# Weight sums by accumulating transfers in two of four query and key steps, and the gate's upper norm ahead of the first step

## The chip, the cores and the metric

The kernel runs on one core of one Trainium2 chip. The metric is the device time of one execution in microseconds, as the median of several runs. One execution was also taken with the hardware profiler; its rows give the times of single instructions.

## The reference

A decoder block on 1024 tokens of width 1024, all in float32. The part around the change is the first projection and what follows it:

```python
xn = rmsnorm(h, norm_mix_g[layer])
proj = xn @ w_in[layer]                       # 1024 x 2568
q, k, v = ...                                 # 512 columns each
log_f = log_sigmoid(proj[..., G_END:] + b_forget[layer])   # 8 columns
att = forgetting_attention(q, k, v, log_f)
uv = gelu(proj[..., V_END:G_END])             # u and vg, 512 columns each
vg = rmsnorm(vg, v_gain)                      # in groups of 64 columns
sg = u * (causal 128x128 mix of vg + b_s)
h = h + concat(att, sg) @ w_out
h = h + conv_ffn(rmsnorm(h, norm_ffn_g), ...) # up, causal depthwise conv, silu gate, down
return rmsnorm(h, norm_final_g)
```

## The kernel before

**Products.** Every large matrix product is cut into 2 x 2 blocks and done with seven block products instead of eight (Strassen-Winograd). The blocks of the weights are called A11, A12, A21, A22 and their sums S1 to S4; those of the activations B11, B21, B22 and T1 to T4. A value that enters a product is split into a high part (a cast on ScalarE) and the rest (a subtraction on VectorE), and a product adds three matmul passes: high by high, high by rest, rest by high. So each weight block or sum costs one operation on ScalarE and one on VectorE before TensorE can use it (`tsplit`). The split tiles lie in a ring of six buffers (two "wy", four "whl").

**Order of the first stages.** u, the gate and the values of the lower 512 tokens are projected first (to about 104 us). Then come four steps of queries and keys, `qk_step(0..3)`, each for 128 columns of q and k, with the forget columns (`forget`, `forget_sums`) between, and after them the upper values, the spatial gate and attention. In a step TensorE runs the products S2, S3, A12 (A11 came in the step before), S1, A22 and S4 (L400, `product`), and VectorE combines the banks qa to qd. S3 and A22 add up in one bank (qc), S1 and S4 in another (qd): the second product of a bank can start only when VectorE has read the first out of it. `emit` scales, splits and stores q and k.

**Weights of a step.** `Weights(i)` loads four blocks of 128 x 512 into two "raw" tiles (of four): `a` holds the blocks 2 and 3 (A11, A12), `b` the blocks 0 and 1 (A21, A22). `sums` makes on GpSimd S3 = A21 + A11 over A11, S2 = S3 + A22 in a "gg" buffer (of two) and S1 = A21 + A22 over A21; `last_sum` makes S4 = S2 + A12 over A12. A sum in place must wait until the block it overwrites has been split. The generator `nxt_of(i)` does this for step i + 1 in the course of step i.

**The gate.** `vgt[0]` and `vgt[1]` hold the gate of the first and of the last 512 tokens ("lower" and "upper" half), each as four tiles of 128 tokens by 512 columns. `gate_part(i)` squares two of the four tiles (ScalarE) and sums the squares over groups of 64 (VectorE) in step i; the second part of a half (i = 1 and i = 3) also takes root and reciprocal and multiplies the half, 2048 wide (tile names G and gms in the profile). `gate_gain` multiplies a half by the gain (G and gg): the upper one in step 3, the lower one after the steps. The gain is loaded into a "gg" buffer and stays there until both are done.

**Values.** After the steps, `wvr[k]` loads the value weights into "raw" tiles as W2 and W3 leave them, and L684 adds the two blocks of each on GpSimd.

**What sets the order.** ScalarE and VectorE keep the written order up to `values_low(3)`. From there a planner orders the instructions of each engine and queue: it goes by their place in the program and by when, by its own costs, their operands and buffers come free. The order on each engine is then fixed. A queue (SP's for loads and stores, GpSimd's) stands still at an instruction whose operands aren't there, and all behind it waits.

In the profile, operations of ScalarE and VectorE in this stage all have the line L43, that of a helper; they are told apart by their tiles (raw and gg into wy or whl: splits; pt: squares and `xu`; qa to qd: banks).

Of the kernel before, what the change touches and what calls it, by code (L numbers as in the profile page):

```python
# [12 lines left out]
ALU = mybir.AluOpType  # L13
AX = mybir.AxisListType
P = 128
# [49 lines left out]
def block_kernel(ctx: ExitStack, tc: tile.TileContext, xT, xtok, wuv, wv, wqk, wf, cpk, bfv,  # L65
                 ggain, g2r, gfr, wsp, woa, wos, wup, wdn, out):
    nc = tc.nc
    act, dve, pool, pe, sp = Line(nc.scalar, tc), Line(nc.vector, tc), Line(nc.gpsimd, tc), nc.tensor, nc.sync
# [13 lines left out]
    def nm(s):  # L82
        uid[0] += 1
        return f"{s}_{uid[0]}"
# [6 lines left out]
    def sb(tag, shape, dt=F32):  # L91
        return (raws if tag == "raw" else late if tag in LATE else early).tile(shape, dt, tag=tag, bufs=BUFS[tag], name=nm(tag))
# [7 lines left out]
    def sbank():  # L100
        return psa.tile([P, 512], F32, tag="s", name=nm("ps"))

    def f32(ap):
        return ap.bitcast(F32)
# [92 lines left out]
    def ring(dt=F32R):  # L197
        rn[0] += 1
        return sb(RTAG[(rn[0] - 1) % 6], [P, 2, 512], dt)

    def psq(tag):
        return psa.tile([P, 512], F32, tag="b" if tag in "ab" else "s", bufs=4, name=nm("q" + tag))
# [29 lines left out]
    for p_ in range(2):  # L232
        t = sb("G", [P, 2, 2, 512])
# [3 lines left out]
    vgt = [sb("G", [P, 4, 512]) for _ in range(2)]  # L237
# [21 lines left out]
    def tprod(banks, src, n, first, neg=False):  # L259
        for k in range(4):  # L260
            tmul(banks, tsplit(src(k), neg), n, k, first)
# [67 lines left out]
    for j in range(2):  # L329
        g = gb[2 * j:2 * j + 2]  # L330
# [3 lines left out]
    for j in range(2):  # L334
        t1, t2, t3 = tmp[j]
        for c in range(2):
            k = 2 * j + c
# [27 lines left out]
    for j in range(2):  # L365
        t2 = tmp[j][1]
        for c in range(2):
            k = 2 * j + c
# [26 lines left out]
    def product(ps, w, n, first):  # L395
        c = 0
        for k in range(4):
            ks = slice(k * P, (k + 1) * P)
            for wi, xi in ((0, 0), (0, 1), (1, 0)):
                pe.matmul(ps, w[:, wi, ks], xs(n, xi, k), start=(first and c == 0), stop=(c == 11),  # L400
                          skip_group_check=True)
                c += 1

    class Weights:


        def __init__(self, i):
            self.a, self.b = sb("raw", [P, 2, 512]), sb("raw", [P, 2, 512])
            sp.dma_start(out=self.a, in_=wqk[i, :, 2:4, :])
            sp.dma_start(out=self.b, in_=wqk[i, :, 0:2, :])  # L410
            self.w = {}
            self.src = {"A11": self.a[:, 0, :], "A12": self.a[:, 1, :], "A22": self.b[:, 1, :]}
# [5 lines left out]
        def sums(self):  # L418

            a11, a21, a22 = self.a[:, 0, :], self.b[:, 0, :], self.b[:, 1, :]  # L420
            s2_ = sb("gg", [P, 512])
            pool.tensor_tensor(out=a11, in0=a21, in1=a11, op=ALU.add)
            pool.tensor_tensor(out=s2_, in0=a11, in1=a22, op=ALU.add)
            pool.tensor_tensor(out=a21, in0=a21, in1=a22, op=ALU.add)
            self.src.update({"S3": a11, "S2": s2_, "S1": a21})

        def last_sum(self):

            a12 = self.a[:, 1, :]
            pool.tensor_tensor(out=a12, in0=self.src["S2"], in1=a12, op=ALU.add)  # L430
            self.src["S4"] = a12

    W = [Weights(0)]
# [54 lines left out]
    def forget_sums(c, r, zr):  # L488
        sel, bfb, z, e, rows = c[0:64, 128:136], c[:, 136:144], c[:, 144:208], c[:, 208:272], c[0:64, 272:400]
        tri, ones, lh, ll = r[:, 0:P], r[:, P:2 * P], r[:, 256:320], r[:, 320:384]  # L490
        v3 = lambda t: t.rearrange("p (h t) -> p h t", h=8)
        ps = sbank()
        for tt in range(8):
            pe.matmul(ps[:, tt * 8:(tt + 1) * 8], zr[:, tt * P:(tt + 1) * P], sel, start=True, stop=True)
        dve.tensor_tensor(out=v3(z), in0=ps[:, 0:64].rearrange("p (t h) -> p h t", h=8),
                          in1=rstd1.unsqueeze(1).to_broadcast((P, 8, 8)), op=ALU.mult)
        dve.tensor_tensor(out=v3(z), in0=v3(z), in1=bfb.unsqueeze(2).to_broadcast((P, 8, 8)), op=ALU.add)
        dve.scalar_tensor_tensor(out=e, in0=z, scalar=-1.0, in1=z, op0=ALU.mult, op1=ALU.max)
        act.activation(e, e, AF.Exp, scale=-1.0)
        act.activation(e, e, AF.Ln, bias=one[:, 0:1])  # L500
        dve.tensor_scalar(out=z, in0=z, scalar1=-1.0, scalar2=0.0, op0=ALU.mult, op1=ALU.max)
        dve.tensor_tensor(out=z, in0=z, in1=e, op=ALU.add)
        dve.tensor_copy(lh, z)
        dve.tensor_tensor(out=ll, in0=z, in1=f32(lh), op=ALU.subtract)

        for o, m in ((64, tri), (128, ones)):
            pe.matmul(ps[:, o:o + 64], m, lh, start=True, stop=False)
            pe.matmul(ps[:, o:o + 64], m, ll, start=False, stop=True)
        whole, run = v3(ps[:, 128:192]), v3(e)
        dve.memset(run[:, :, 0:1], 0.0)  # L510
        for tt in range(1, 8):
            dve.tensor_tensor(out=run[:, :, tt:tt + 1], in0=run[:, :, tt - 1:tt], in1=whole[:, :, tt - 1:tt], op=ALU.add)
        dve.tensor_tensor(out=v3(z), in0=v3(ps[:, 64:128]), in1=run, op=ALU.add)
        pe.transpose(ps[0:64, 192:320], z, ident)
        act.activation(rows, ps[0:64, 192:320], AF.Copy, scale=-1.0)
        sp.dma_start(out=ncd.rearrange("h (t p) -> (h t) p", p=P), in_=rows)
# [12 lines left out]

    gms = cst.tile([P, 64], F32, name="gms")  # L530

    def gate_part(i):

        hf, t = 1 - i // 2, 2 * (i % 2)
        sq = sb("pt", [P, 2, 512])
        act.activation(sq, vgt[hf][:, t:t + 2, :], AF.Square)
        r = gms[:, hf * 32 + t * 8:hf * 32 + t * 8 + 16]
        dve.tensor_reduce(out=r, in_=sq.rearrange("p t (g d) -> p (t g) d", d=64), axis=AX.X, op=ALU.add)
        if t:
            r = gms[:, hf * 32:hf * 32 + 32]  # L540
            act.activation(r, r, AF.Sqrt, bias=eps[:, 0:1], scale=1.0 / 64)
            dve.reciprocal(r, r)
            v3 = vgt[hf].rearrange("p t (g d) -> p (t g) d", d=64)
            dve.tensor_tensor(out=v3, in0=v3, in1=r.unsqueeze(2).to_broadcast((P, 32, 64)), op=ALU.mult)

    def nxt_of(i):
        if i == 3:
# [13 lines left out]
    def qk_step(i, qa, nxt):  # L561
        w, t = W[i], xu[i]
        x1, u2 = t[:, 0, :], t[:, 1, :]
        qb = psq("b")
        product(qb, w.w["S2"], "T2", True)
        next(nxt)
        dve.tensor_tensor(out=u2, in0=qb, in1=x1, op=ALU.subtract)
        qc = psq("c")
        product(qc, w.w["S3"], "T3", True)
        dve.tensor_tensor(out=tk[:, 1, hi], in0=u2, in1=qc, op=ALU.subtract)  # L570
        w.split("S1")
        if i > 0:
            product(qa, w.w["A12"], "B21", False)
            act.copy(tq[:, 1, lo], qa)
        else:
            dve.tensor_tensor(out=tq[:, 1, lo], in0=q2, in1=x1, op=ALU.add)
        emit(tq, qd, i, -0.125, (lo,))
        w.split("A22")
        if i == 3:
            gate_gain(1)  # L580
        qd_ = psq("d")
        product(qd_, w.w["S1"], "T1", True)
        dve.tensor_tensor(out=tk[:, 1, hi], in0=tk[:, 1, hi], in1=qd_, op=ALU.subtract)
        gate_part(i)
        product(qc, w.w["A22"], "T4", False)
        dve.tensor_tensor(out=tk[:, 1, lo], in0=u2, in1=qc, op=ALU.subtract)
        emit(tk, kd, i, 1.0, (lo, hi))
        qa = next(nxt)
        w.split("S4")
        next(nxt)  # L590
        product(qd_, w.w["S4"], "B22", False)
        dve.tensor_tensor(out=tq[:, 1, hi], in0=qd_, in1=u2, op=ALU.subtract)
        emit(tq, qd, i, -0.125, (hi,))
        return qa

    gg = []

    def gate_gain(hf):
        if not gg:
            gg.append(sb("gg", [P, 512]))  # L600
            sp.dma_start(out=gg[0], in_=ggain.to_broadcast((P, 512)))
        dve.tensor_tensor(out=vgt[hf], in0=vgt[hf], in1=gg[0].unsqueeze(1).to_broadcast((P, 4, 512)), op=ALU.mult)

    W[0].split("S2", "S3")
    forget_sums(*fg)
    for i in range(4):
        qa = qk_step(i, qa, nxt_of(i))
# [2 lines left out]
    wvr = []  # L610
    for k in range(4):
        t = sb("raw", [P, 2, 512])
        sp.dma_start(out=t, in_=wv[k])
        wvr.append(t)


# [25 lines left out]
    for p_ in range(2):  # L642
        t = ring(F32)
# [37 lines left out]
    S = [sbank() for _ in range(4)]  # L681
    for k in range(4):
        tmul(S, w0[k], "T3", k, True)
        pool.tensor_tensor(out=wvr[k][:, 1, :], in0=wvr[k][:, 0, :], in1=wvr[k][:, 1, :], op=ALU.add)  # L684
    tprod(S, lambda k: wvr[k][:, 1, :], "B22", False)
    spatial()
    for m in range(4):
# [495 lines left out]
    for p_, n in ((upl, "B11"), (upl, "T2"), (upl, "B21"), (upl, "T3"), (upr, "T1"), (upr, "T4"), (upr, "B22")):  # L1183
        t = ut_(p_, "x" + n, [P, 2, 4, 512], F32, 1)
# [37 lines left out]
    def blk(b):  # L1222
        return lambda p_: wd[p_][:, b, :]
# [129 lines left out]
```

## Time and profile before

| | us |
|---|---|
| median of 3 runs | 1100.56 (1096.5 to 1100.8) |
| the profiled execution, its own time | 1103.27 |
| its span, first to last instruction | 1101.5 |
| TensorE busy with matmuls | 1073.1 (97%) |
| VectorE busy | 900.0 (82%) |
| ScalarE busy | 572.7 (52%) |
| GpSimd busy | 249.2 (23%) |

The four steps lie at 118.4, 137.8, 156.8 and 176.1 us, the upper values from 200.2 us. A row of a timeline gives the start, the length (of all that it holds), the engine, the line, what is written and read, how often, and in brackets the idle time before it with what ended it. The release that it names is the one that came last by the profile; where that can't be the reason, the program tells which it was. A product's twelve matmuls overlap, so the distance from one product's start to the next one's is its price, not the length in the row.

### The profile page before, as it was taken

How to read it: one execution, taken by the hardware profiler on the slowest of the kernel's cores; microseconds unless marked ns; L12 is line 12 of the kernel's file. 1: busy time of each engine (PE TensorE's matmuls, PEld its weight loads, DVE VectorE, ACT ScalarE, POOL GpSimd, SP SyncE). 2: the span in 40 equal slices, each digit the busy share in tenths (PEclk: the TensorE clock that was granted, in tenths of full speed). 3: DMA queues.
4: the chain of work that ended last, by engine and by line, in shares of the span. 5: the costliest groups of instructions: out<-in, count | busy, mean ns of one | idle time of the engine just before them, and what ended most of it. 6: DMA issues, size and time to landing. Idle time of an engine off the chain costs nothing.

```text
span 1101.5 us, 14438 instructions
## 1 busy us (share of the span) xinstructions
PE 1073.1 (97%) x5013; PEld 881.8 (80%) x5013; DVE 900.0 (82%) x1355; ACT 572.7 (52%) x991; POOL 249.2 (23%) x205
## 2 busy tenths in 40 slices
PE   9999999999998999988999999999999999999997
PEld 6888787777887888766888888888888888888886
DVE  5985799775678977999798989999998876898774
ACT  6656544454468865653444444444444454454653
POOL 0002243133035331334232423333232000000000
PEclk9999999899999999999999999999999999999999
DMA  9242366846548345113123232313321899433342
GB/s 339 85 153 78 100 169 181 231 140 209 189 133 268 98 144 188 70 67 134 68 105 134 78 114 96 124 68 123 116 96 45 270 330 324 122 97 101 124 137 96
DMA packets 64714, 158.18 MB, mean 144 GB/s; under 512 B 7673, under 2 KB 7937, under 8 KB 64641
## 3 DMA queue, kind: packets, MB, share of 16 engines
q1 hardware_dynamic: 64352, 156.70, 42.5%
q8 instruction: 39, 0.64, 0.2%
q10 hardware_dynamic: 288, 0.56, 0.1%
q14 instruction: 35, 0.28, 0.1%
HBM read 114.95 MB, written 42.27 MB: 143 GB/s over the span
## 4 chain that ended last, share of the span: by engine, by line
PE 67%; DVE 7%; ACT 3%; DMA 2%; issue 2%; POOL 1%; SPq 0%; DVEq 0%; ACTq 0%; POOLq 0%
PE k L1210 18%; PE qd L1020 10%; PE qa L1020 10%; PE qc L1020 9%; PE qb L1020 5%; PE pb L794 2%; PE ps L256 2%; PE pb L784 2%; PE pf L824 1%; PE pf L823 1%; PE pf L825 1%; DVE whb L159 1%; DMA rsd<-t 1%; PE ps L759 1%; PE ps L758 1%
## 5 line engine op out<-in xcount | busy, mean ns | idle before, releaser
L1210 PE MATMUL k<-whb,wha 128*128 128x512 f32 x924 | 209.6, 389 | 0.0
L1210 PEld LDWEIGHTS k<-whb,wha 128*128 128x128 f32 x924 | 173.4, 188 | 36.1
L1020 PE MATMUL qa<-xB,wha 128*128 128x512 f32 x528 | 129.4, 395 | 5.7 <-DVE wha L159 5.7
L1020 PE MATMUL qc<-xT,whb 128*128 128x512 f32 x540 | 130.3, 390 | 1.7 <-DVE xT L951 1.3
L1020 PEld LDWEIGHTS qa<-xB,wha 128*128 128x128 f32 x528 | 100.2, 190 | 27.3 <-DVE wha L159 6.5
L1020 PEld LDWEIGHTS qc<-xT,whb 128*128 128x128 f32 x540 | 101.1, 188 | 23.8 <-DVE xT L951 1.8
L153 ACT CAST wha<-sg 128x512 fp32r<-128x512 f32 x77 | 47.9, 622 | 97.3 <-PE k L1210 87.1
L153 ACT CAST whb<-sg 128x512 fp32r<-128x512 f32 x85 | 52.0, 616 | 70.3 <-PE qc L1020 67.7
L159 DVE TENSOR_TENSOR wha<-sg,wha 128x512 fp32r<-128x512 f32 x77 | 52.9, 689 | 42.5 <-ACT wha L153 42.4
L159 DVE TENSOR_TENSOR whb<-sg,whb 128x512 fp32r<-128x512 f32 x85 | 63.0, 742 | 8.9 <-ACT whb L153 8.7
L1020 PE MATMUL qd<-xB,whb 128*128 128x512 f32 x264 | 64.6, 393 | 0.1
L794 PE MATMUL pb<-pt,V 128*128 128x256 f32 (+1 forms) x320 | 60.1, 301 | 4.6 <-ACT pt L785 4.0
L1020 PE MATMUL qd<-xT,whb 128*128 128x512 f32 x264 | 63.4, 389 | 0.0
L1020 PE MATMUL qb<-xT,whb 128*128 128x512 f32 x252 | 61.0, 389 | 1.0 <-DVE whb L159 1.0
L794 PEld LDWEIGHTS pb<-pt,V 128*128 128x128 f32 x320 | 48.0, 192 | 16.6 <-ACT pt L785 11.4
L785 ACT CAST pt<-pb 128x512 fp32r<-128x512 f32 (+1 forms) x80 | 41.0, 543 | 36.7 <-PE pb L784 36.0
L786 DVE TENSOR_TENSOR pt<-pb,pt 128x512 fp32r<-128x512 f32 (+1 forms) x80 | 48.6, 634 | 13.3 <-ACT pt L785 12.8
L1020 PEld LDWEIGHTS qd<-xB,whb 128*128 128x128 f32 x264 | 50.2, 190 | 11.0 <-issue 0.5
L1020 PEld LDWEIGHTS qd<-xT,whb 128*128 128x128 f32 x264 | 49.6, 188 | 10.3
L908 POOL TENSOR_TENSOR sg<-sg,raw 128x512 f32<-128x512 f32 x21 | 42.8, 2038 | 64.7 <-issue 61.3
L907 POOL TENSOR_TENSOR sg<-raw 128x512 f32<-128x512 f32 x21 | 30.7, 1460 | 112.7 <-DVE whb L159 103.4
L1020 PEld LDWEIGHTS qb<-xT,whb 128*128 128x128 f32 x252 | 47.2, 188 | 11.2 <-DVE whb L159 1.4
(391 smaller groups left out, 2310.8 us busy)
## 6 DMA issues: line engine op xcount, KB each, us to landing
raw<-wup SPq DMA_DIRECT2D x44, 512.0 KB, 3.6
sg<-hx SPq DMA_DIRECT2D x77, 256.0 KB, 3.0
hx<-hs SPq DMA_DIRECT2D x44, 256.0 KB, 2.0
hx<-ca SPq DMA_DIRECT2D x33, 256.0 KB, 2.2
xT<-wdn SPq DMA_DIRECT2D x28, 256.0 KB, 5.3
raw<-wqk SPq DMA_DIRECT2D x8, 512.0 KB, 3.3
qd<-G SPq DMA_DIRECT2D x16, 256.0 KB, 3.3
kd<-G SPq DMA_DIRECT2D x16, 256.0 KB, 3.2
```

Source lines behind the costliest of these rows:

```text
L153: act.copy(h, src)
L159: return eng.tensor_tensor(out=l, in0=src, in1=f32(h), op=ALU.subtract)
L256: pe.matmul(banks[m], xs(n, xi, k)[:, ms], w[:, wi, :], start=(first and k == 0 and c == 0), stop=(k == 3 and c == 2), skip_group_check=True)
L758: pe.matmul(ps[:, 0:e - c], A[:, qs], B[:, c:e], start=True, stop=False)
L784: pe.transpose(ptr[:, c:c + P], tj[jj][:, k * P:(k + 1) * P], ident)
L785: act.copy(pt[:, 0, 0:w], ptr[:, 0:w])
L786: dve.tensor_tensor(out=pt[:, 1, 0:w], in0=ptr[:, 0:w], in1=f32(pt[:, 0, 0:w]), op=ALU.subtract)
L794: pe.matmul(po[:, oo:oo + n], lhs, pt[:, s, o:o + n], start=(k == 0 and s == 0), stop=(s == 1 and half))
L907: pool.tensor_tensor(out=s[0], in0=a21, in1=a22, op=ALU.add)
L908: pool.tensor_tensor(out=s[1], in0=s[0], in1=a11, op=ALU.add)
L1020: pe.matmul(ps, w[:, wi, ks], xb[:, xi, k, :], start=(first and n == 0), stop=(n == 11), skip_group_check=True)
L1210: pe.matmul(banks[bk + m], xh[:, xi, ms], wh[:, wi, :], start=(first and p_ == 0 and n == 0), stop=(p_ == NP - 1 and n == 2), skip_group_c ...
```

## The change

- In steps 2 and 3 the weight sums aren't made by GpSimd's adds. S2's buffer is loaded with block 2 by a plain transfer from SP's queue, and transfers issued by GpSimd add block 0 and block 1 to it, block 1 to A21 (S1) and block 0 to A11 (S3), all from memory. S4 is made by a transfer that adds S2, from one buffer to the other, to A12. Steps 0 and 1 keep the adds.
- The upper value sums are made by an accumulating transfer behind each load, instead of L684.
- The upper half's two gate parts (with its norm) stand ahead of step 0, before `forget_sums`; the lower half's stand in the steps 0 and 1 instead of 2 and 3. The gain of the upper half stands in step 2 instead of 3.
- The multiplications by norm and gain are cut into two pieces of 1024 each.

```diff
         def __init__(self, i):
-            self.a, self.b = sb("raw", [P, 2, 512]), sb("raw", [P, 2, 512])
+            self.i, self.a, self.b = i, sb("raw", [P, 2, 512]), sb("raw", [P, 2, 512])
...
             s2_ = sb("gg", [P, 512])
-            pool.tensor_tensor(out=a11, in0=a21, in1=a11, op=ALU.add)
-            pool.tensor_tensor(out=s2_, in0=a11, in1=a22, op=ALU.add)
-            pool.tensor_tensor(out=a21, in0=a21, in1=a22, op=ALU.add)
+            if self.i < 2:
+                pool.tensor_tensor(out=a11, in0=a21, in1=a11, op=ALU.add)
+                pool.tensor_tensor(out=s2_, in0=a11, in1=a22, op=ALU.add)
+                pool.tensor_tensor(out=a21, in0=a21, in1=a22, op=ALU.add)
+            else:
+                blk = lambda b: wqk[self.i, :, b, :]
+                sp.dma_start(out=s2_, in_=blk(2))
+                for t, b in ((s2_, 0), (a21, 1), (s2_, 1), (a11, 0)):
+                    pool.dma_start(out=t, in_=blk(b), accum_op=ALU.add)
             self.src.update({"S3": a11, "S2": s2_, "S1": a21})
...
             a12 = self.a[:, 1, :]
-            pool.tensor_tensor(out=a12, in0=self.src["S2"], in1=a12, op=ALU.add)
+            if self.i < 2:
+                pool.tensor_tensor(out=a12, in0=self.src["S2"], in1=a12, op=ALU.add)
+            else:
+                pool.dma_start(out=a12, in_=self.src["S2"], accum_op=ALU.add)
...
-    def gate_part(i):
-
-        hf, t = 1 - i // 2, 2 * (i % 2)
+    def gate_part(hf, t):
+
         sq = sb("pt", [P, 2, 512])
...
-            v3 = vgt[hf].rearrange("p t (g d) -> p (t g) d", d=64)
-            dve.tensor_tensor(out=v3, in0=v3, in1=r.unsqueeze(2).to_broadcast((P, 32, 64)), op=ALU.mult)
+            for t in (0, 2):
+                v3 = vgt[hf][:, t:t + 2, :].rearrange("p t (g d) -> p (t g) d", d=64)
+                dve.tensor_tensor(out=v3, in0=v3, in1=r[:, t * 8:t * 8 + 16].unsqueeze(2).to_broadcast((P, 16, 64)),
+                                  op=ALU.mult)
...
         w.split("A22")
-        if i == 3:
-            gate_gain(1)
         qd_ = psq("d")
         product(qd_, w.w["S1"], "T1", True)
         dve.tensor_tensor(out=tk[:, 1, hi], in0=tk[:, 1, hi], in1=qd_, op=ALU.subtract)
-        gate_part(i)
+        if i < 2:
+            gate_part(0, 2 * i)
+        elif i == 2:
+            gate_gain(1)
...
-        dve.tensor_tensor(out=vgt[hf], in0=vgt[hf], in1=gg[0].unsqueeze(1).to_broadcast((P, 4, 512)), op=ALU.mult)
+        for t in (0, 2):
+            v = vgt[hf][:, t:t + 2, :]
+            dve.tensor_tensor(out=v, in0=v, in1=gg[0].unsqueeze(1).to_broadcast((P, 2, 512)), op=ALU.mult)

     W[0].split("S2", "S3")
+    gate_part(1, 0)
+    gate_part(1, 2)
     forget_sums(*fg)
...
         sp.dma_start(out=t, in_=wv[k])
+        pool.dma_start(out=t[:, 1, :], in_=wv[k, :, 0, :], accum_op=ALU.add)
         wvr.append(t)
...
         tmul(S, w0[k], "T3", k, True)
-        pool.tensor_tensor(out=wvr[k][:, 1, :], in0=wvr[k][:, 0, :], in1=wvr[k][:, 1, :], op=ALU.add)
```

## The prediction

> **What bounds the kernel now.** I read the page first, then the stage that the diff touches: a table by steps, TensorE's waits there, and the order of time on each engine.
>
> ```profile
> span 1101.5 us, 14438 instructions
> PE 1073.1 (97%) x5013; PEld 881.8 (80%) x5013; DVE 900.0 (82%) x1355; ACT 572.7 (52%) x991; POOL 249.2 (23%) x205
> ```
>
> TensorE is busy 97% of the span, so only what shortens its path counts: 28 us are idle, and some matmuls run slowly. The windows view (span; busy time and count of PE, PEld, DVE, ACT, POOL; granted clock; DMA share; GB/s), cut at the first matmul of the steps 1, 2, 3 and of the value products:
>
> ```profile
> 137.80:156.80 19.00, 19.00 (x85) 15.73 (x84) 17.48 (x23) 8.80 (x15) 8.21 (x4) 1.00 0.59 158
> 156.80:176.10 19.30, 19.30 (x86) 15.69 (x85) 17.92 (x19) 6.84 (x12) 9.78 (x6) 1.00 0.55 154
> 176.10:200.20 24.10, 19.29 (x74) 15.15 (x73) 22.21 (x27) 12.81 (x23) 4.47 (x3) 0.87 0.70 201
> 200.20:222.50 22.30, 22.30 (x98) 18.45 (x97) 14.78 (x22) 8.75 (x14) 3.37 (x5) 0.98 0.86 254
> ```
>
> Steps 1 and 2 are full of matmuls. Step 3 takes 24.10 us for fewer of them (74), at a clock of 0.87, with VectorE busy 22.21 of 24.10 us. So the loss is in step 3 and VectorE is late there. TensorE's waits from 104 to 225 us (line, releaser: total, times, longest) hold nothing else of size:
>
> ```profile
> PE qd L400 <- ACT G L43: 4.1, 1, 4.1
> PE ps L507 <- DVE gg L43: 0.8, 1, 0.8
> PE qc L400 <- DVE G L43: 0.7, 1, 0.7
> ```
>
> The timeline of PE (start, length, group, and in brackets the idle time before it):
>
> ```profile
> 156.81 2.88 PE L400 MATMUL qb<-H,whl 128*128 128x512 f32 x12
> ...
> 176.09 2.88 PE L400 MATMUL qb<-H,wy 128*128 128x512 f32 x12
> 178.81 2.88 PE L400 MATMUL qc<-x,wy 128*128 128x512 f32 x12
> ...
> 184.25 2.88 PE L400 MATMUL qd<-H,whl 128*128 128x512 f32 x12
> 187.84 2.96 PE L400 MATMUL qc<-V,whl 128*128 128x512 f32 x12 [0.71 <-DVE G L43]
> 194.91 5.46 PE L400 MATMUL qd<-t,whl 128*128 128x512 f32 x12 [4.11 <-ACT G L43]
> 200.17 6.00 PE L256 MATMUL ps<-wy,x 128*128 128x512 f32 x24
> ```
>
> A product follows the one before after 178.81 - 176.09 = 2.72 us. Step 3 has six products (S2, S3, A12, S1, A22, S4), 16.32 us, and takes 200.17 - 176.09 = 24.08. The 7.76 us of loss lie in three places: A22 starts 187.84 - 184.25 - 2.72 = 0.87 late, S4 starts 194.91 - 187.84 - 2.72 = 4.35 late, and S4 itself, after that idle time, takes 200.17 - 194.91 = 5.26, so 2.54 too long. What S4 waited for is on VectorE:
>
> ```profile
> 180.48 1.22 DVE L43 TENSOR_REDUCE gms<-pt 128x16 f32<-128x1024 f32 x1 [0.27 <-ACT pt L43]
> ...
> 182.21 0.34 DVE L43 RECIPROCAL gms<-gms 128x32 f32<-128x32 f32 x1
> ...
> 183.02 2.28 DVE L43 TENSOR_TENSOR G<-G,gms 128x2048 f32<-128x2048 f32 x1
> ...
> 187.01 0.68 DVE L43 TENSOR_TENSOR G<-pt,qc 128x512 f32<-128x512 f32 x1
> 187.61 2.67 DVE L43 SCALAR_TENSOR_TENSOR wy<-raw,wy 128x512 fp32r<-128x512 f32 x2
> 190.20 2.28 DVE L43 TENSOR_TENSOR G<-G,gg 128x2048 f32<-128x2048 f32 x1
> 192.40 1.77 DVE L43 SCALAR_TENSOR_TENSOR G<-G,t 128x512 f32<-128x512 f32 x1
> 194.09 0.67 DVE L43 TENSOR_TENSOR G<-G,qd 128x512 f32<-128x512 f32 x1
> 194.69 0.68 DVE L43 SCALAR_TENSOR_TENSOR whl<-raw,whl 128x512 fp32r<-128x512 f32 x1
> ```
>
> S4 accumulates on bank qd, which the subtraction at 194.09 must have read: it ends at 194.76, and S4 starts 0.15 later. The wait view names ScalarE because a cast ended last; the program says VectorE. A22 likewise stands behind the subtraction of qc at 187.01. VectorE has no gap in this stretch, so these two reads are late by whatever stands ahead of them: the gate's second norm (reduction, reciprocal, multiplication), and adds of GpSimd beside them:
>
> ```profile
> 142.39 3.37 DVE L43 TENSOR_TENSOR G<-G,gms 128x2048 f32<-128x2048 f32 x1
> ```
> ```profile
> 143.57 3.35 POOL L424 TENSOR_TENSOR raw<-raw 128x512 f32<-128x512 f32 x1
> ...
> 151.40 1.61 POOL L430 TENSOR_TENSOR raw<-gg,raw 128x512 f32<-128x512 f32 x1 [4.48 <-DVE wy L43]
> ...
> 188.19 1.55 POOL L654 TENSOR_SCALAR_AFFINE_SELECT pt<-pt 128x1024 f32<-128x1024 f32 x1
> 192.35 1.26 POOL L684 TENSOR_TENSOR raw<-raw 128x512 f32<-128x512 f32 x1 [2.62 <-DMA raw<-wv]
> ```
>
> The same multiplication took 3.37 us beside the add at 143.57 and 2.28 without one: 1.09 more. GpSimd's add suffers too, 3.35 us there and 1.26 at 192.35. The operation at 192.40 (1.77, where the one at 194.69 takes 0.68) pays the same 1.09, beside the add at 192.35.
>
> **The change part by part.** *Step 3's norm goes.* The part of the gate that ran in step 3 now runs in step 1, and the upper half's norm runs ahead of step 0. Out of step 3 go 1.22 + 0.34 + 2.28 = 3.84 us of VectorE. *Its adds go:* L684 becomes four transfers, so the operation at 192.40 is 1.09 shorter. The two splits at 187.61 (2.67 for two of 0.68) may gain up to 1.3, but the select at 188.19 stays beside them, and I take 0. The subtraction of qd then starts at 194.09 - 3.84 - 1.09 = 189.16, ends at 189.83, and S4 may start at 189.98. A22 no longer waits: 184.25 + 2.72 = 186.97, to 189.69. So S4 is still 0.29 late. A gap of 0.87 cost its product 0.08 (2.96 against 2.88), so I take 0.1 for its clock. S4 ends at 189.98 + 2.72 + 0.1 = 192.8 instead of 200.17: **7.4 us gained**. Next to be late is VectorE again; the value products behind S4 are fed by splits that come the same 4.93 us earlier.
>
> *The norm in front* adds, ahead of step 0, one more square on ScalarE, a reduction, a root with its table load, a reciprocal and the multiplication. One reduction ran there already:
>
> ```profile
> 112.17 1.22 DVE L43 TENSOR_REDUCE gms<-pt 128x16 f32<-128x1024 f32 x1 [0.70 <-ACT pt L43]
> ...
> 120.41 0.23 DVE L43 TENSOR_TENSOR gg<-ps,rstd 128x64 f32<-128x64 f32 x1 [3.91 <-PE ps L494]
> ```
> ```profile
> 111.08 1.06 ACT L43 ACTIVATE pt<-G 128x1024 f32<-128x1024 f32 x1 [0.34 <-issue]
> ...
> 121.10 1.28 ACT L43 ACT_TABLE_LOAD   x1
> ```
>
> On VectorE that is 1.22 + 0.34 + 2.28 = 3.84 us, and there is a gap of 3.91 us just before 120.41. Its cover is that gap. Behind it stands the forget chain, whose end TensorE awaited for 0.8 us (L507). If one reduction comes first, that wait grows by up to 1.2; at best the 0.8 goes. I take the middle, **0.2 lost**. ScalarE's 1.06 and 1.28 find room on an engine that is busy 52% of the span. Cutting the multiplications into halves lets the planner put short operations between and costs nothing that a row shows. The gain's multiplication of the upper half already ran in step 2, so moving its line changes little; its load now comes earlier and holds one of the two "gg" buffers.
>
> *The sums of steps 2 and 3 by transfers.* This is the unknown: nothing in this trace accumulates in a transfer or is issued by GpSimd. Per step there is a plain load of block 2 into S2's buffer and five accumulations of 256 KB, of which three are a chain: S2 += block 0, S2 += block 1, S4 += S2. Call one A, issue to landing. The nearest rows, and SP's queue (the DMA rows end with the size and the us to landing):
>
> ```profile
> raw<-xtok SPq DMA_DIRECT2D x16, 256.0 KB, 3.1
> ...
> x<-kd SPq DMA_DIRECT2D x16, 256.0 KB, 8.0
> ...
> ncd<-gg SPq DMA_DIRECT2D x1, 32.0 KB, 1.8
> ```
> ```profile
> 133.01 0.47 SPq L516 DMA_DIRECT2D ncd<-gg  x1
> 133.74 4.30 SPq L528 DMA_DIRECT2D kd<-G  x4
> ...
> 153.58 4.41 SPq L528 DMA_DIRECT2D kd<-G  x4
> ```
>
> A lies between 1.8 and 8.0. A plain load of that size lands in 3.1, and an accumulation reads two operands and needs GpSimd's issue, which I put near one GpSimd add (1.26): I take 4.5. By the Trainium skill (DMA: Bandwidth & Descriptors, section "Anatomy of one DMA — SWDGE (gpsimd) path") such a transfer takes 2.0 us plus its bytes over 436 GB/s, 2.6 us here by my estimate, and the sum would be the same; no row here shows it.
>
> W2's S2 buffer comes free when the forget rows are stored (133.01 + 1.8 = 134.8), and SP is at kd until 138.0. So its load lands at 138.0 + 3.1 = 141.1, the sum at 141.1 + 2A = 150.1, and a split (a cast and a subtraction, 0.7 each as at 187.01) makes it ready at 151.5, where TensorE wants it at 156.81. S4 needs A12 to be split, which is so at 151.40, so it lands at 155.9. That frees the buffer which W3's S2 must take, since the gain sits in the other one. SP is at kd until 158.0; load 161.1; sum 170.1; ready at 171.5, wanted at 176.09. **With A = 4.5 this costs nothing, and 4.6 us are to spare.** Waiting for it: the splits of ScalarE and VectorE behind it, on SP the stores of q and k behind the load, and on GpSimd the next accumulations. With A over 5.1 S4 waits for S2, and W3's S2 is ready at 141.1 + 2A + A + 3.1 + 2A + 1.4 = 145.6 + 5A: late from A = 6.1, and each us more costs 5. The accumulations of the values follow loads that land in step 3, and their sums are split only after four value products have run: covered.
>
> Sum: -7.4 + 0.2 = -7.2. The profiled execution took 1103.27 us, so 1096.1; against the median of 1100.56 that is **1093.4 us**.
>
> **The rivals.** *GpSimd is held up in issuing.* If it is slowed beside VectorE as its add was (3.35 against 1.26, 2.1 more), A is 6.6 and W3's S2 is ready at 178.6, 2.5 late; with some slow clock after the gap (between 0.1 and 2.54, say 1.1) 3.6 of the 7.2 come back: 1097. For it: VectorE is busy nine tenths of these steps. Against: only the issue would stretch, not the landing. The Trainium skill (same page, section "SWDGE vs HWDGE vs iDMA") says that GpSimd writes the descriptors into SBUF, the state that VectorE locks it out of in one of its modes; no run here shows it yet. A smaller part of the backlog going, for another order by the planner, gives about the same time.
>
> *The accumulations are too slow, and the kernel is slower.* Place: W2's S2, S4, then W3's S2. The DMA share is already 0.55 to 0.59 in steps 1 and 2, and 0.70 in step 3; five accumulations and a load come on top, and kd's loads landed in 8.0 in a busy stretch. With A = 9, W3's S2 is ready at 190.6, 14.5 late, and the clock costs 2.5 more: 17.0 - 7.2 = +9.8, about 1110. It decides from 145.6 + 5A - 176.09 + 2.5 - 7.2 = +5.5, that is A = 8.1. Against: that is above the slowest kind of 256 KB row here.
>
> *It doesn't do what it says.* The planner sets the late operations, the value splits and the gain, ahead of the two reads anyway, and VectorE fills the place with them: 1100. Against: these already stand ahead of them in this trace.
>
> **How the numbers follow.** The forecast has 0.54, its own range 1090 to 1096 (front and the splits beside the select: 1.3 more, 1.2 less, and about 1 for another order elsewhere). GpSimd held up or half a gain: 0.18, at 1095 to 1101. Nothing: 0.06. Too slow: 0.22, from 1106 up, mostly near 1110. A measurement tells about 0.5%, 5.5 us. Faster by more (under 1095): the forecast and a little of the second case, 0.55; within: 0.22; slower: 0.23. The range from 1089 to 1108 leaves out most of the slow case and little below.
>
> **What would show it.** Right: in step 3 no wait of qd over 0.5 us, the clock near 1.00, value products from about 193; no add of GpSimd after 140 us except W1's; VectorE's multiplications by gms and gg of 1.1 to 1.2 us each, without one of 3.37. For A: the time from GpSimd's issues to landing, under 6. Wrong: ScalarE waiting long for a transfer into gg, and after it TensorE waiting on S2 at the start of step 2 or 3; SP idle in front of the load into gg with the stores behind it; or a wait at L507 well over 0.8.

## The result and the profile after

The changed kernel is slower: 1109.5, 1111.1 and 1117.75 us against a median of 1098.5 (1096.4 to 1100.8) of the kernel before on the same chip, a ratio of 1.0129 with a 95% interval of 1.0105 to 1.0153. (A fourth execution took 2743 us and is left out as disturbed.) The forecast was 1093.4. The profiled execution is the one of 1117.75 us. From its page, the head, the busy times and the two queues:

```profile
span 1116.0 us, 14462 instructions
...
PE 1077.2 (97%) x5013; PEld 883.9 (79%) x5013; DVE 890.8 (80%) x1359; ACT 575.1 (52%) x992; POOL 239.9 (21%) x207
...
q1 hardware_dynamic: 64640, 157.22, 42.9%
q0 software_dynamic: 2016, 3.67, 2.0%
```

VectorE and GpSimd have less to do than before (900.0 and 249.2 us), and the span is 14.5 us longer. So the time went into waits. The windows view, cut as before at the first matmul of the steps 1, 2 and 3, of the upper values and of the spatial gate (so S2's wait in step 2 falls into the first row):

```profile
137.80:162.00 24.20, 19.51 (x86) 15.50 (x84) 15.14 (x23) 6.93 (x12) 5.29 (x7) 0.98 0.85 200
162.00:185.30 23.30, 22.02 (x85) 17.59 (x85) 14.02 (x20) 5.66 (x11) 5.18 (x6) 0.88 0.88 209
185.30:206.60 21.30, 17.27 (x72) 13.37 (x73) 17.99 (x30) 12.90 (x24) 2.68 (x4) 1.00 0.75 205
206.60:232.70 26.10, 23.69 (x97) 19.08 (x96) 13.94 (x20) 8.96 (x14) 4.03 (x5) 0.93 0.90 269
```

Steps 1 and 2, which were full (19.0 and 19.3), now take 24.2 and 23.3; step 3 takes 21.3, better than 24.1 and far from the 16.3 that its six products need; the values take 26.1 instead of 22.3. VectorE is no longer full in any of them. The DMA share of steps 1 and 2 went from 0.59 and 0.55 to 0.85 and 0.88. TensorE's waits from 100 to 240 us, and the products behind them in the timeline of PE:

```profile
PE qb L400 <- ACT whl L43: 4.5, 1, 4.5
PE qc L400 <- DVE G L43: 2.6, 1, 2.6
PE ps L256 <- DVE G L43: 2.4, 1, 2.4
PE qd L400 <- DVE G L43: 1.6, 2, 1.4
PE qb L400 <- ACT wy L43: 1.3, 1, 1.3
PE ps L523 <- DVE gg L43: 0.7, 1, 0.7
```
```profile
162.00 5.49 PE L400 MATMUL qb<-H,whl 128*128 128x512 f32 x12 [4.51 <-ACT whl L43]
167.28 3.12 PE L400 MATMUL qc<-x,wy 128*128 128x512 f32 x12
...
185.28 3.33 PE L400 MATMUL qb<-H,wy 128*128 128x512 f32 x12 [1.28 <-ACT wy L43]
188.44 2.89 PE L400 MATMUL qc<-x,wy 128*128 128x512 f32 x12
...
199.40 3.00 PE L400 MATMUL qc<-V,whl 128*128 128x512 f32 x12 [2.63 <-DVE G L43]
203.79 3.00 PE L400 MATMUL qd<-t,whl 128*128 128x512 f32 x12 [1.39 <-DVE G L43]
```

The first wait is new and the largest: the first product of step 2 (S2) starts 4.51 us late and then takes 167.28 - 162.00 = 5.28 us instead of 2.72. The first product of step 3 comes 1.28 late. In step 3 both old waits remain, 2.63 for qc and 1.39 for qd. The queue of SP, GpSimd's issues and ScalarE's waits in that stretch show where S2 was (L428 loads block 2 into S2's buffer, L430 adds the blocks, L439 adds S2 to A12, L537 is `emit`'s store, L525 the store of the forget rows, L612 loads the gain):

```profile
136.36 0.48 SPq L525 DMA_DIRECT2D ncd<-gg  x1
137.34 2.88 SPq L537 DMA_DIRECT2D kd<-G  x3
142.38 1.23 SPq L537 DMA_DIRECT2D qd<-G  x2
143.73 0.61 SPq L428 DMA_DIRECT2D gg<-wqk  x1
...
156.96 7.58 SPq L537 DMA_DIRECT2D kd<-G  x4
164.63 0.75 SPq L612 DMA_DIRECT2D gg<-ggain  x1
165.49 0.95 SPq L428 DMA_DIRECT2D gg<-wqk  x1
```
```profile
149.71 0.87 POOL L430 DMA_DIRECT2D gg<-wqk  x1 [4.72 <-DMA gg<-wqk]
154.79 0.88 POOL L430 DMA_DIRECT2D gg<-wqk  x1 [4.22 <-DMA gg<-wqk]
...
161.92 0.86 POOL L439 DMA_DIRECT2D raw<-gg  x1 [5.35 <-DMA gg<-wqk]
```
```profile
161.33 0.62 ACT L43 CAST whl<-gg 128x512 fp32r<-128x512 f32 x1 [5.12 <-DMA gg<-wqk]
...
184.61 0.62 ACT L43 CAST wy<-gg 128x512 fp32r<-128x512 f32 x1 [8.75 <-DMA gg<-wqk]
```

W2's chain reads: load issued 143.73, first accumulation 149.71, second 154.79, landed 161.33, split, and S2's product at 162.00. Only then can S4's transfer go (161.92). W3's load into the buffer (165.49) needs S4's transfer to be done, and it also stands in SP's queue behind the stores of k, the last of which wait for VectorE's late work and take until 164.54, and the gain's load. Its sum lands at 184.61. ScalarE stands in its order before each of these casts, 5.12 and 8.75 us, and VectorE's splits behind it.

Two more profiled executions, one of each kernel on one chip, show how much of this repeats. The changed kernel again, unaltered:

> The changed kernel again, one look: the wait for S2 at step 2 (4.5 us in the first profile) and the value products' start near 206 us are the same within 1 us; the part behind the steps, 883 us in the first profile, is where the executions differ, 876 to 880 here.

The kernel before again, unaltered:

> The kernel before again, one look: step 3 loses 7.8 us as in the first profile if that loss is fixed by the order; less, 4 to 6 us, if the adds beside VectorE fall differently from execution to execution, which would explain why the gate's move alone gained nothing in the median.

| us from the span's start | before | before again | after | after again |
|---|---|---|---|---|
| S2 product of step 1 | 137.8 | 137.8 | 137.8 | 137.9 |
| S2 product of step 2 | 156.8 | 156.9 | 162.0 | 162.1 |
| S2 product of step 3 | 176.1 | 176.1 | 185.3 | 184.6 |
| first value product | 200.2 | 198.0 | 206.6 | 206.1 |
| spatial gate | 222.3 | 219.8 | 232.7 | 230.6 |
| from there to the end | 879.2 | 878.6 | 883.3 | 876.2 |

The changed kernel repeats its wait for S2 (4.2 us). Up to the spatial gate it is 10.4 and 10.8 us behind. The part behind, which the change doesn't touch, lies between 874 and 883 us in the fourteen profiled executions, so some us of the first execution's 1117.75 are probably not the change's. The kernel before lost 198.0 - 176.1 - 16.3 = 5.6 us in its step 3 this time, not 7.8:

```profile
PE qd L400 <- DVE G L43: 1.9, 1, 1.9
PE qc L400 <- DVE G L43: 1.6, 1, 1.6
```

So the loss from which the forecast started was 2.1 us larger in the one execution profiled than in another.

### The profile page after: what moved, and what is told of

Same layout as the page of the kernel before. It is cut to its first block, busy times and chain, and to the rows that moved or that the text cites. A ratio compares the mean times of both kernels' runs of the same rounds, so it can differ in the third digit from the quotient of the medians.

```text
span 1116.0 us, 14462 instructions
## 1 busy us (share of the span) xinstructions
PE 1077.2 (97%) x5013; PEld 883.9 (79%) x5013; DVE 890.8 (80%) x1359; ACT 575.1 (52%) x992; POOL 239.9 (21%) x207
## 3 DMA queue, kind: packets, MB, share of 16 engines
q1 hardware_dynamic: 64640, 157.22, 42.9%
q0 software_dynamic: 2016, 3.67, 2.0%
## 4 chain that ended last, share of the span: by engine, by line
PE 77%; DVE 9%; DMA 6%; ACT 3%; issue 2%; POOL 1%; SPq 0%; DVEq 0%; ACTq 0%; POOLq 0%
PE k L1225 18%; PE qd L1035 9%; PE qa L1035 9%; PE qc L1035 9%; PE ps L256 6%; PE pb L256 5%; PE qb L1035 5%; PE pb L809 3%; DMA gg<-wqk 3%; PE pb L799 2%; DVE G L43 1%; PE pf L839 1%; PE pf L840 1%; PE pf L838 1%; DMA x<-kd 1%
## 5 line engine op out<-in xcount | busy, mean ns | idle before, releaser
L1035 PEld LDWEIGHTS qb<-xT,whb 128*128 128x128 f32 x252 | 47.2, 188 | 11.1 <-DVE whb L159 1.4
```

Of the source, the lines that this page charges most:

```text
L1035: pe.matmul(ps, w[:, wi, ks], xb[:, xi, k, :], start=(first and n == 0), stop=(n == 11), skip_group_check=True)
```

## The experiments

**Theory:** S2's chain of three transfers is late, since the gate's norm in front delays its start and each transfer takes longer than forecast. **Rivals:** the gate's move alone is the loss; the value transfers are; the "gg" buffer that the gain holds from step 2 on makes W3's load late; the accumulating itself, not the queueing, is the price. Ratios are to the kernel before, with 95% intervals; diffs are against the changed kernel. The condition `self.i < 2` stands in two places, in `sums` and in `last_sum`; where a diff changes the first, the run changes both.

**One part at a time.** The gate's moves and pieces alone, all sums by adds:

```diff
-            if self.i < 2:
+            if self.i < 4:
...
-        pool.dma_start(out=t[:, 1, :], in_=wv[k, :, 0, :], accum_op=ALU.add)
...
+        pool.tensor_tensor(out=wvr[k][:, 1, :], in0=wvr[k][:, 0, :], in1=wvr[k][:, 1, :], op=ALU.add)
```

> The gate's move and its pieces alone; all sums by GpSimd's adds as before. Chain theory (the change lost by its serial transfers, and the gate's move is worth what was predicted, less the 1.09 us of an add beside VectorE): step 3's wait of qd falls from 4.1 us to under 1.5, the clock of step 3 is near 1.00, time 6 us under the kernel before, ratio 0.994. Rival (the norm in front costs what it saves, by one more table load and a later forget chain): ratio 0.999 to 1.005. Rival (transfers load the queues): same as the chain theory here.

Measured 0.9999 (0.9981 to 1.0017), so my 0.994 was missed. The value products start at 196.1, 2 to 4 us earlier than before, but step 2 is now longer, 177.2 - 156.2 = 21.0. This kernel's timeline of PE has, in step 2:

```profile
168.70 3.01 PE L400 MATMUL qc<-V,whl 128*128 128x512 f32 x12 [1.47 <-DVE G L43]
```

VectorE's lateness moved to the step in which the gain now stands, and 1.9 us of waiting for qd stay in step 3. The spatial gate starts at 219.7, as in the second execution of the kernel before (219.8): at the value products TensorE now waits 1.51 us for a bank.

The sums of steps 2 and 3 by transfers alone; gate and values as before (the lines that make the gate's multiplications whole again and put the gain back in step 3 are left out of the diff):

```diff
-        if i < 2:
-            gate_part(0, 2 * i)
-        elif i == 2:
-            gate_gain(1)
+        gate_part(i)
...
-    gate_part(1, 0)
-    gate_part(1, 2)
...
-        pool.dma_start(out=t[:, 1, :], in_=wv[k, :, 0, :], accum_op=ALU.add)
...
+        pool.tensor_tensor(out=wvr[k][:, 1, :], in0=wvr[k][:, 0, :], in1=wvr[k][:, 1, :], op=ALU.add)
```

> The sums of steps 2 and 3 by transfers alone; gate and value sums as before. Chain theory: TensorE waits for S2 at the start of step 2 (4 to 5 us) and near step 3, with slow clock behind each, and the gate's backlog of step 3 is partly hidden behind these; slower than the whole change or like it, ratio 1.012 to 1.020. Rival (the gate's move is the cost): ratio 1.000 to 1.005. Rival (transfers load the queues): ratio 1.008 to 1.012, less than the whole change, since four of fourteen accumulations are gone.

Measured 1.0033 (1.0016 to 1.0051), far less than I expected. It lies where the rival on the gate's move had it, but that move alone costs nothing (0.9999). The queue of SP and ScalarE's cast of S2 in this kernel:

```profile
133.23 0.48 SPq L525 DMA_DIRECT2D ncd<-gg  x1
134.02 4.74 SPq L537 DMA_DIRECT2D kd<-G  x4
138.88 0.61 SPq L428 DMA_DIRECT2D gg<-wqk  x1
```
```profile
155.40 0.62 ACT L43 CAST whl<-gg 128x512 fp32r<-128x512 f32 x1 [7.09 <-DMA gg<-wqk]
```

The chain takes 155.40 - 138.88 = 16.5 us, about as long as in the changed kernel (161.33 - 143.73 = 17.6). But it starts 4.85 us earlier and is just in time: TensorE doesn't wait for S2. What it pays instead is 4.2 us of waiting for qc in step 2: VectorE reads qc late, since its work follows the late split of S2 (156.06) and since it waits 1.22 us for the gain's load.

The value sums by transfers alone, all else as before (the gate's other lines left out as above):

```diff
-            if self.i < 2:
+            if self.i < 4:
...
-        if i < 2:
-            gate_part(0, 2 * i)
-        elif i == 2:
-            gate_gain(1)
+        gate_part(i)
...
-    gate_part(1, 0)
-    gate_part(1, 2)
```

> The value sums by accumulating transfers alone. Chain theory: these transfers have no successor that TensorE awaits; one add beside VectorE is gone (1.09 us), ratio 0.998 to 1.000. Rival (transfers load the queues, which delays the stores and loads around 180 to 200 us): ratio 1.003 or more.

Measured 0.997 (0.9951 to 0.9988), a gain of 3.2 us in the medians, more than the 0.998 to 1.000 that I expected. The gate and the values together, the sums of all steps by adds:

```diff
-            if self.i < 2:
+            if self.i < 4:
```

> The gate's move and the value sums by transfers; the sums of the steps by adds. Chain theory: everything that was predicted without the chain, 7 us faster, ratio 0.993 to 0.994, so all of the loss and more lies in the transfers of steps 2 and 3. Rival (gate's move costs): 0.999 or more. Rival (queues): 0.997 or more.

Measured 0.9975 (0.9956 to 0.9993), a miss too: I had expected 0.993 to 0.994. TensorE waits 1.45 us for qc in step 2, as with the gate's moves alone. So the whole change without the transfers of the steps is worth -0.25%, the transfers of the steps alone +0.33%, and all together +1.29%: the parts don't add up, they collide.

**The chain.** The same sums with two transfers in S2's chain instead of three (S1 is added up first, and S2 takes it from A21's buffer):

```diff
-                for t, b in ((s2_, 0), (a21, 1), (s2_, 1), (a11, 0)):
-                    pool.dma_start(out=t, in_=blk(b), accum_op=ALU.add)
+                for t, s in ((a21, blk(1)), (s2_, a21), (a11, blk(0))):
+                    pool.dma_start(out=t, in_=s, accum_op=ALU.add)
```

> The whole change, but S2 is block 2 plus S1, added from A21's buffer once S1 has landed there, so two serial transfers (load and one accumulation, from a buffer: 3.7 us in the changed kernel) instead of three (5.4 + 4.6 + 6.5 and 5.3 + 6.9 + 5.6). Chain theory: S2 of step 2 is split before 156 and its wait of 4.5 us goes; what is left is at most 1 us at step 3; ratio 0.998 to 1.003. Rival (the accumulations are slow because they load the DMA queues): one transfer of eleven less, ratio 1.009 or more.

Measured 1.0022 (1.0008 to 1.0036), as expected: TensorE no longer waits for S2, and 1.07% of the 1.29% is gone. What is left is more than the 1 us that I allowed: waits for qd, 3.8 us, behind splits that still wait for transfers: ScalarE's longest are 8.0 for W3's S2 and 5.4 for a sum of W2.

**The gain and its buffer.** The gain back in step 3, all else as changed:

```diff
+        if i == 3:
+            gate_gain(1)
...
-        elif i == 2:
-            gate_gain(1)
```

> The whole change, but the gain of the upper half stays in step 3, so its load takes a gg buffer after W3's S2 and not ahead of it. Buffer theory (the two halves of the change meet in the gg buffers, which is why each alone costs so little): W3's load into gg is issued near 146 us, as with the transfers alone, instead of 165.5, and nothing waits for S2 at step 3; step 2's wait of 4 to 5 us stays, since W2's load isn't moved; ratio 1.004 to 1.009. Rival (it is the length of W2's chain alone, the rest follows from it): W3's load stays behind W2's S4 or comes early without effect, ratio 1.011 or more.

Measured 1.009 (1.0067 to 1.0114), inside the range that I gave the buffer theory, but not for its reason: with a buffer to spare W3's load still comes at 164.22 instead of near 146, behind the stores of k that W2's lateness delays. The wait for S2 in step 2 stays (3.88). At the start of step 3 it is gone, and a wait of 2.95 us for qd stands just ahead of that instead. So the buffer isn't what makes W3's load late. The 0.4% gained is about what the same move of the gain is worth without the steps' transfers (0.9975 against 0.994, below). The same with the short chain:

```diff
-                for t, b in ((s2_, 0), (a21, 1), (s2_, 1), (a11, 0)):
-                    pool.dma_start(out=t, in_=blk(b), accum_op=ALU.add)
+                for t, s in ((a21, blk(1)), (s2_, a21), (a11, blk(0))):
+                    pool.dma_start(out=t, in_=s, accum_op=ALU.add)
...
+        if i == 3:
+            gate_gain(1)
...
-        elif i == 2:
-            gate_gain(1)
```

> Both: S2 from S1, and the gain in step 3. Chain and buffer theory: no wait for S2 in step 2 or 3, step 3 without a long wait, the value products from 193 to 195 us; ratio 0.995 to 0.999. Rival (DMA queues loaded by accumulations): 1.004 or more.

Measured 1.0012 (0.9993 to 1.0031), a miss: no gain even with a short chain and an early load (154.83). This kernel's ScalarE and PE:

```profile
151.52 0.62 ACT L43 CAST wy<-raw 128x512 fp32r<-128x512 f32 x1 [4.97 <-DMA raw<-wqk]
...
174.58 0.62 ACT L43 CAST wy<-raw 128x512 fp32r<-128x512 f32 x1 [5.30 <-DMA raw<-wqk]
```
```profile
178.40 5.43 PE L400 MATMUL qd<-t,whl 128*128 128x512 f32 x12 [4.24 <-DVE G L43]
```

What is late now are sums in A21's and A11's buffers: each may start only when its block has been split, and by the chain view two of them, issued at 143.89 and 163.43, take 7.6 and 11.1 us to land. ScalarE waits for them about 5 us a step, and once TensorE waits 4.24 us for a bank behind that and pays for a slow product again.

**Only step 3 by transfers** (the threshold for both sums one step higher):

```diff
-            if self.i < 2:
+            if self.i < 3:
```

> The whole change, but step 2's sums by GpSimd's adds; only step 3's are transferred. If the late S2 of step 2 is what starts the loss: no wait at step 2's start, W3's load into gg before 160 us, a wait of at most 2 us at step 3's start; ratio 0.998 to 1.004. If each step's transfers cost alike: ratio 1.004 to 1.008. If the loss is step 3's own: 1.009 or more.

Measured 1.0002 (0.9985 to 1.0019), as expected. On top of the gate and the values (0.9975), step 3's transfers cost 0.003, and step 2's another 0.013.

**Accumulating or queueing?** The same transfers as plain copies. The block sums of steps 2 and 3 are left out here, so only its time says something; each engine and queue has the same order as in the changed kernel:

```diff
-                    pool.dma_start(out=t, in_=blk(b), accum_op=ALU.add)
+                    pool.dma_start(out=t, in_=blk(b))
...
-                pool.dma_start(out=a12, in_=self.src["S2"], accum_op=ALU.add)
+                pool.dma_start(out=a12, in_=self.src["S2"])
```

> The whole change with the accumulations of the steps 2 and 3 turned into plain copies by the same queue (block sums of these steps are left out: S1 to S4 are copies of single blocks); the same waits, and the order on every engine is unchanged. If the accumulating itself makes the transfers long (two reads, 2.0 percent of the engines' span for 3.67 MB, twice the price of the other queue's bytes): each falls from 6 us to about 4, W2's S2 comes 4 to 5 us sooner, its wait falls under 1.5 us and the ratio to 0.999 to 1.005. If the length is GpSimd's issue and the busy queues: the copies take 5.5 us or more and the ratio stays at 1.009 or more.

Measured 1.0063 (1.0039 to 1.0086), between the two theories. Its waits, DMA issues and queue:

```profile
PE qb L400 <- ACT whl L43: 4.1, 1, 4.1
```
```profile
q0 software_dynamic: 1376, 3.67, 1.3%
...
gg<-wqk POOLq DMA_DIRECT2D x4, 256.0 KB, 5.7
```

The wait for S2 is still 4.1 us: without any adding, the chain that starts at 143.8 lands at 160.5. The copies take about as long as the queueing theory had them, but the ratio falls below its 1.009. So about half of the loss is queueing and the late start. The other half comes with the adding, and in these profiles most of it lies behind S2: step 3 starts at 182.5 instead of 185.3, the values at 202.9 instead of 206.6.

**The part that works.** Sums by adds, values by transfers, the upper norm ahead of step 0, the gain back in step 3:

```diff
-            if self.i < 2:
+            if self.i < 4:
...
+        if i == 3:
+            gate_gain(1)
...
-        elif i == 2:
-            gate_gain(1)
```

> Sums of the steps by adds; values by transfers; upper norm ahead of step 0; gain in step 3. If moving the gain into step 2 cost 1.5 us there (a wait of qc that the gate's move alone showed), that wait goes and the ratio is 0.994 to 0.996. If VectorE's work in step 3 is what counts, the gain's 2.3 us there brings the wait of qd back and the ratio is 0.997 to 0.999, no better than the value transfers alone.

Measured 0.994 (0.992 to 0.9959), 1092.8 us: this beats both kernels, as expected. Its step 3 in the windows view, VectorE's read of qd, and PE's S4 and first value product:

```profile
176.00:192.50 16.50, 16.50 (x73) 13.44 (x72) 15.81 (x27) 11.16 (x21) 2.86 (x3) 1.00 0.81 224
```
```profile
188.86 0.69 DVE L43 TENSOR_TENSOR G<-G,qd 128x512 f32<-128x512 f32 x1
```
```profile
189.69 2.97 PE L400 MATMUL qd<-t,whl 128*128 128x512 f32 x12
192.50 2.20 PE L256 MATMUL ps<-wy,x 128*128 128x512 f32 x9
```

Step 3 is full, at a clock of 1.00, and the values start at 192.50.

## Why the prediction was wrong

**Right in the place and the cause, by luck in the size: the loss in step 3.** VectorE's backlog made S4 late, and without the norm and the adds in step 3 the loss is gone. The forecast had VectorE's read of qd at 189.16, S4 at 189.98 and its end at 192.8; the last experiment shows 188.86, 189.69 and 192.50. But the two terms behind it were mis-sized. The value transfers alone, with the norm still in step 3, bring this read to 190.31, where the two executions of the kernel before have 194.09 and 192.79. That is 2.5 to 3.8 us for the adds; the forecast gave them 1.09. It counted only the add at 192.35. The kernel before has four such adds, and one in step 2 slows the gain's multiplication there, so that all of VectorE's work behind it comes later. Before:

```profile
166.06 3.37 DVE L43 TENSOR_TENSOR G<-G,gg 128x2048 f32<-128x2048 f32 x1
```
```profile
165.54 1.73 POOL L684 TENSOR_TENSOR raw<-raw 128x512 f32<-128x512 f32 x1
```

With the value transfers alone:

```profile
166.26 2.28 DVE L43 TENSOR_TENSOR G<-G,gg 128x2048 f32<-128x2048 f32 x1
...
190.31 0.67 DVE L43 TENSOR_TENSOR G<-G,qd 128x512 f32<-128x512 f32 x1
```

The norm's 3.84 us, in turn, came to less: from 190.31 to 188.86, with all of the gate's moves, are 1.45 us. Other work takes its place. Five splits of the gate (`H<-G,H`, 0.6 us each), the first of which the kernel before runs only at 198.90, stand ahead of the read of qd in the last experiment.

**Missed: the gain's place.** "Moving its line changes little" was wrong. With it in step 2 the kernel with gate and values runs at 0.9975, with it in step 3 at 0.994 (the two intervals just touch), without the wait for qc in step 2. The planner runs the gain's multiplications in step 2 even so, but the first at 163.87 instead of 154.17.

**Mis-sized: the base.** 7.76 us stood in one execution, 5.6 in another.

**Right for TensorE, missed beside it: the norm in front.** Step 1 starts at 137.82 against 137.76, so TensorE lost no more than the forecast 0.2, and the wait of the forget chain (L523 now) is 0.7 instead of 0.8. But the forget rows are stored at 136.36 instead of 133.01. The prediction named their store as the thing that frees S2's buffer, and didn't ask what the norm ahead of it does to it.

**The step that failed: the transfers.** W2's S2, by the terms of the sum:

| W2's S2, us | forecast | after |
|---|---|---|
| load issued | 138.0 | 143.73 |
| load to first accumulation's issue (landing) | 3.1 | 5.98 |
| two accumulations | 9.0 | 11.62 |
| landed | 150.1 | 161.33 |

A came out at 11.62 / 2 = 5.8, inside its bounds of 1.8 to 8.0 and below 6.1, from which my formula let W3's S2 be late. With A of 5.8 alone, the formula has W2's S2 in time, and W3's at 145.6 + 29 = 174.6, in time too. What it lacked is the 143.73 - 138.0 = 5.7 us by which the load starts late, and 2.9 us of its landing. I took SP to be free for the load once kd was issued. The stores of k now take until 140.2, and the planner put the load behind q's next store too (142.38), which waits for VectorE. Without the gate's moves and the value transfers the load stands ahead of that store (138.88 against 142.47), and a chain about as long (16.5 us) is in time. W3's load then follows W2's late work, through the stores of k and the buffer, and TensorE waits for S2 again at the start of step 3.

**The rivals.** "Too slow" had the right place (W2's S2, S4, then W3's S2) and about the right time (1110), but decided "from A = 8.1"; with the late start it decided far below. "GpSimd is held up in issuing": no; a single issue took 0.86 to 0.89 us in steps 1 to 3 and one right behind another 1.20, beside a VectorE that was at work or not. The Trainium skill (DMA: Bandwidth & Descriptors, "SWDGE vs HWDGE vs iDMA") would have allowed longer issues beside VectorE; no row here shows one. "It doesn't do what it says" wasn't the loss, but its mechanism shows: the planner fills the place in step 3 with late work. In the changed kernel VectorE first waits 2.27 us for the split of S4, and then three of the splits `H<-G,H` stand ahead of its read of qc (198.58) and five ahead of that of qd (202.97); TensorE waits for both reads.

**The signs named beforehand.** The multiplications by norm took 1.2 us a piece, and no 3.37 is left: right. "ScalarE waiting long for a transfer into gg, then TensorE waiting on S2 at the start of step 2 or 3" is what the profile shows, in both.

**The values.** "Covered" held without the steps' transfers (0.997 alone). In the changed kernel the chain view runs through S4's transfer and a plain load of value weights, which the kernel before has too:

```profile
189.62 3.98 DMA raw<-gg
...
197.62 6.18 DMA raw<-wv
```

At the value products TensorE then waits 2.41 us for the bank of S4, which VectorE reads at 210.51. This wait isn't tied to the value transfers: it is 1.51 us with the gate's moves alone and 0.76 with the steps' transfers alone.

**Open:** what makes the planner put q's store ahead of the load was not separated. Each kernel whose W2 load starts past 143 us has the upper norm in front, the lower half's parts in steps 0 and 1, and the value transfers, though none of these is issued before 169 us. Nor is it shown why plain transfers from GpSimd's queue land as late as 5.7 us here.

## What to carry to other kernels

An engine's add that becomes a chain of transfers trades busy time for latency: price the whole chain from the instruction that frees its first buffer, through the queue that it stands in, and ask what the other parts of the same change do to that instant. Here a set of edits that gains 0.25% alone and one that costs 0.33% alone cost 1.29% together; with the first in place the other's chain starts 4.85 us later and misses its step. And a loss read from one execution can be more than a third larger than in the next (7.8 and 5.6 us): profile a second one before giving a gain its size.

## What the runs showed of the hardware

- **Accumulating transfers cost twice the engine time.** In the changed kernel 3.67 MB on GpSimd's queue took 2.0% of the DMA engines' span, 0.54% a MB; SP's queue took 42.9 / 157.22 = 0.27%. With ten of the fourteen as plain copies the same bytes took 1.3%, which leaves about 0.07% for a copy and 2.0 / 14 = 0.14% for an accumulation. The issue on GpSimd's side is shorter too, 0.54 us a plain copy against 0.87.
- **They land late.** 256 KB from memory, median from issue to landing in the changed kernel:

```profile
raw<-wqk POOLq DMA_DIRECT2D x4, 256.0 KB, 6.7
gg<-wqk POOLq DMA_DIRECT2D x4, 256.0 KB, 6.0
...
raw<-gg POOLq DMA_DIRECT2D x2, 256.0 KB, 3.7
```

  From one buffer to the other it is 3.7. The Trainium skill's fit (DMA: Bandwidth & Descriptors, "Anatomy of one DMA — SWDGE (gpsimd) path"), 2.0 us plus bytes over 436 GB/s, gives an estimate of 2.6 for each; the rows differ, in steps where the DMA share is 0.75 to 0.88, and the measurement decides.
- **A gap on TensorE costs again behind it.** After 4.51 us of idle time the next product took 5.28 us instead of 2.72, at a granted clock of 0.50; after 1.28 us it took 3.16, at a clock of 1.00. The length of the gap alone doesn't decide it: in the second execution of the changed kernel the product after 1.64 us took 4.71, at a clock of 0.64. What decides it isn't shown.
